# Delta net: block inverse issued in a row on VectorE, convolution taps and background products queued behind it, some key-query products in other PSUM banks

## The chip, the core and the metric

The kernel runs on one core of a Trainium2 chip. The core has five engines, each with a queue of its own that it works through in order: PE (TensorE, matmul; its weight loads are listed as PEld), DVE (VectorE), ACT (ScalarE), POOL (GpSimd) and SP (SyncE, which here issues most of the DMAs). An instruction that waits holds up everything behind it on its engine. The metric is the device time of the kernel in microseconds, the median of several executions.

## The reference

Two layers of a transformer trunk over 1024 positions of width 1024. The first layer's mixer is a gated delta net, the second's is retention; behind each stands a gated feed-forward block. The change touches the delta net alone:

```python
qkv = jax.nn.silu(causal_dwconv(qkv, conv_w))          # four taps
...
kk = jnp.where(strict, jnp.einsum('bhncd,bhnmd->bhncm', kb, k) * decay, 0.0)
eye = jnp.eye(C, dtype=F32)
rhs = jnp.concatenate([v * beta[..., None], kb * jnp.exp(gc)[..., None]], axis=-1)
sol = lax.linalg.triangular_solve(kk + eye, rhs, left_side=True, lower=True, unit_diagonal=True)
...
qk = jnp.where(causal, jnp.einsum('bhncd,bhnmd->bhncm', q, k) * decay, 0.0)
...
_, o = lax.scan(step, state0, xs)                       # state passed from chunk to chunk
```

There are 8 heads. For every head and chunk a unit lower triangular matrix has to be inverted (or solved with). Apart from that the layer is a large projection of the input (`h @ w_in`, 4112 columns), a convolution of four taps with a SiLU, key-query products and a scan over chunks.

## The kernel before

**The parts.** The kernel takes chunks of 128 positions, 8 of them. The delta net works on four pairs of heads. For each pair there are: `t_front` (decay and key-key products, which make the matrix `U`), `t_solve` (one for two pairs: inverts all 32 x 32 diagonal blocks of four heads at once), `t_chain` (joins the inverted blocks to inverses of 128 x 128 by small matmuls), `prep` (turns values and keys), `dt_half` (key-query products, multiplied by the decay that is loaded back from DRAM), and `scan`, one per head. Underneath lies `filler`: the projection matmuls, one unit of 128 columns after the other. A unit loads its weights (`load_w`, lines 100 to 106: a DMA into a raw tile `wr`, then ACT rounds it to `wh`, then DVE takes the rest into `wl`), runs 24 matmuls of 128 x 512 for each half of the positions (three for each of eight k tiles, the first of them with `wl`), and, for convolution units, calls `conv_half` on each half.

**Convolution.** `conv_half` (lines 443 to 456) copies the PSUM bank twice on ACT (lines 449 and 452), adds three taps on DVE (line 454) and applies SiLU on ACT (line 455). For query and key units, `ssq_late` comes some time later: it turns the finished features on PE (line 638) and sums their squares on ACT (line 473).

**Background.** `bg_step` at the end of a unit runs one piece of a matrix-vector product that a later stage needs: a DMA of 512 KB into a tile `mvw` and two products on DVE (lines 214 and 216, into `ada`). `mvw` and `wr` share one tag with two buffers, so a piece that waits for its products holds a buffer that raw weights need.

**The inverse.** `t_solve` (lines 785 to 818) copies the blocks into `X` on ACT (line 792), transposes them on DVE to `Y` (line 796), and then does 31 elimination steps, each a product (line 804, into `fs`) and a subtraction (line 806, into `T`), each depending on the one before: 62 instructions in a chain. Then follow the transpose `RX` on DVE (line 810), the reordering copy `TP` on ACT (line 812) and the transpose `TX` on DVE (line 814). `t_chain` copies `RX` into `R` (ACT line 852, POOL line 854) and `TX` into `T0` (ACT line 841). The loads of the decay tiles `DT` for `dt_half` (line 944) go into a buffer that `T` leaves.

**What sets the order.** PE's order in the delta net is written by hand: a small planner (`run`, lines 646 to 680) keeps a clock, advances it by a cost for each matmul, takes the ready stream with the best priority, and pins every matmul behind the one before (`pq`). A stream says by `yield LAT[...]` how long it thinks its work on other engines lasts. In `t_solve` it yields 1.9 us after every second elimination step, so that other streams are traced in between. The order on DVE, ACT, POOL and SP comes from a scheduler, which goes by the order of tracing and by its own estimate of when an operand is ready. `after(key)` (line 94) adds an edge for order only: what is traced inside it, on the same engine as the anchor instruction, is issued behind that instruction. It adds no wait.

**PSUM.** Eight banks: four of tag `acc`, two of `mm`, two of `sc`. `dt_half`, `prep`, `t_front` and `t_chain` use `mm`, the scans use `sc` and `acc`.

Of the kernel before, what the change touches and what calls it, by code (L numbers as in the profile page):

```python
# [12 lines left out]
ALU = mybir.AluOpType  # L13
# [3 lines left out]
D = 1024  # L17
# [16 lines left out]
def trunk_kernel(ctx: ExitStack, tc, A):  # L34
# [84 lines left out]
    def bg_step(tile=mm_tile):  # L119
        bg_ps[0] = tile  # L120
        if bg:
            bg.pop(0)()
# [38 lines left out]
    for k in range(KT):  # L161
        w = two("hTa", F32, "mvw")
# [17 lines left out]
    pt = col_sum([a0])  # L180
# [262 lines left out]
    def conv_half(tile_idx, acc, half, o, prev):  # L443
        raw = tl("cv", [P, 516], name="raw")
        if half == 0:
            pool.memset(raw[:, 0:3], 0.0)
        else:
            pool.tensor_copy(raw[:, 0:3], prev[:, HALF:HALF + 3])
        act.activation(raw[:, 3:515], acc, AF.Copy)
        w = gdn_cw[:, tile_idx * 4:tile_idx * 4 + 4]  # L450
        oh = o[half]
        act.activation(oh, acc, AF.Copy, scale=w[:, 3:4])  # L452
        for j in range(1, 4):
            dve.scalar_tensor_tensor(oh, raw[:, 3 - j:515 - j], w[:, 3 - j:4 - j], oh, ALU.mult, ALU.add)  # L454
        act.activation(oh, oh, AF.Silu)
        return raw

# [237 lines left out]
    def give(tag, n):  # L695
        free[tag] += n
# [88 lines left out]
    def t_solve(qd_):  # L785
        yield after_ev(("T0", 2 * qd_ - 1), ("A", 2 * qd_), ("A", 2 * qd_ + 1))
        yield from take("lane", 1)
        X = tl("lane", [P, 32, 32], name="X")
        for h in pairs[2 * qd_] + pairs[2 * qd_ + 1]:
            for b in range(4):  # L790
                bs = slice(32 * b, 32 * b + 32)
                act.activation(X[bs, :, h % 4 * 8:h % 4 * 8 + 8].rearrange("p i c -> p c i"), U[h][bs, :, bs], AF.Copy)
        yield from take("lane", 2)
        yield LAT["X"]
        Y = tl("lane", [P, 32, 32], name="Y")
        dve.transpose(flat(Y), flat(X))
        T = tl("lane", [P, 32, 32], name="T")
        pool.memset(T, 0.0)
        pool.memset(flat(T)[:, 0:1024:33], 1.0)
        tmp = tl("fs", [P, 256], name="fs")  # L800
        for j in range(31):
            ni, nj = 31 - j, j + 1
            tv = tmp[:, 0:ni * nj].rearrange("p (i j) -> p i j", j=nj)
            dve.tensor_tensor(tv, bc(Y[:, j + 1:, j], nj), bm(T[:, j, 0:nj], ni), ALU.mult)
            ts_ = T[:, j + 1:, 0:nj]
            dve.tensor_tensor(ts_, ts_, tv, ALU.subtract)
            if j % 2:
                yield LAT["fs"]
        RX = tl("lane", [P, 32, 32], name="RX")
        dve.transpose(flat(RX), flat(T))  # L810
        TP = tl("lane", [P, 32, 32], name="TP")
        act.activation(TP, T.rearrange("p i j -> p j i"), AF.Copy)
        TX = tl("lane", [P, 32, 32], name="TX")
        dve.transpose(flat(TX), flat(TP))
        RTX[qd_] = (RX, TX)
        give("lane", 1)
        emit(("Tq", qd_))
        emit(("T", qd_), LAT["T"])
# [111 lines left out]
    def dt_half(p, q4):  # L930
        heads = pairs[p]
        if q4 == 0:
            yield after_ev(("Tq", p // 2), ("M", p - 1))
            yield from take("lane", 1)
            t = tl("lane", [P, 2, HALF], name="DT")
            tiles = [t[:, 0], t[:, 1]]
        else:
            yield after_ev(("Tq", p // 2), ("S", p - 1))
            yield from take("auh", 2)
            emit(("Dt", p))  # L940
            tiles = [tl("auh", [P, HALF], name="DT") for _ in range(2)]
        for h, t in zip(heads, tiles):
            DT[h, q4] = t
            sp.dma_start(t, Ld[h][:, hs(q4)])
        yield LAT["ld"]
        for h, t in zip(heads, tiles):
            yield after_ev(("f", h))
            pt = mm_tile()
            for c in range(4):
                n = q4 * 4 + c  # L950
                pm(pt[:, c * P:(c + 1) * P], fx(GH + h, n), fx(h, n))
            dve.tensor_tensor(t, t, pt, ALU.mult)
            emit(("D", h, q4), LAT["D"])
            yield LAT["mm"]
# [92 lines left out]
    def filler(items):  # L1047
        spare = [(z, k) for k in range(GH)]
        todo = list(items)
        while todo or spare:  # L1050
# [34 lines left out]
            if kind == "c":  # L1085
                if ti < GH:
                    yield [(0.2, ssq_late(ti))]
                else:
                    emit(("f", ti), LAT["fv"])
            bg_step(acc_tile)  # L1090

    LAT = {"kk": 3.05, "ld": 1.14, "g1": 17.30, "gm": 2.50, "mm": 1.81, "T": 4.98, "X": 3.38, "fs": 1.9, "T0": 5.00, "t1": 1.65, "t2": 2.35, "t3": 1.34, "D": 2.67, "s1": 1.60, "s2": 1.22, "s3": 1.26, "tail": 12.31, "ssq": 9.30, "fv": 2.85}
# [829 lines left out]
```

## Time and profile before

| | |
|---|---|
| median of 3 runs | 3016.57 us (3015.99 to 3017.25) |
| the profiled execution | 3017.08 us, of which the profile's span is 3015.3 us |
| mean granted clock of PE | 0.975 |
| busy share of the span, VectorE | 73% (2196.9 us) |
| busy share of the span, ScalarE | 45% (1349.4 us) |
| DMA, mean rate | 147 GB/s |
| elimination steps (lines 804 and 806) | 62 instructions each, over both inverses |
| first inverse, start of first and last step | 178.9 and 222.1 us |
| second inverse, start of first and last step | 428.5 and 474.7 us |

The times of rows are counted from the start of the span. A row of the timeline gives start, duration, engine, line, operation, operands and the number of instructions merged, and in brackets how long the engine had been idle before it and what ended that idle time. A row of a window gives, for each engine, the busy time and in parentheses the number of instructions, then the granted clock of PE (1.00 is full speed), the DMA share and rate.

### The profile page before, as it was taken

Reading aid. Unit: us, or ns where it says so; the run is one execution under the profiler, and the core shown is the slowest. Engines: PE = TensorE matmul, PEld = TensorE weight load, DVE = VectorE, ACT = ScalarE, POOL = GpSimd, SP = SyncE. Lnnn points to the kernel's source line nnn. Section 1 sums busy time; section 2 is a strip of 40 time slices with the busy share of each in tenths; the row PEclk is TensorE's granted clock in tenths of the full one; section 3 lists DMA queues with packets and bytes.
Section 4 is the critical chain, followed back from the end, with each engine's and each line's share of the span. In section 5 each row is a group of like instructions: output and inputs, shape, how many; then the busy total and the mean of one; then the engine's idle time right before and its main releaser. Section 6 shows DMA issues by size and latency. Waiting matters only on the chain.

```text
span 3015.3 us, 38927 instructions
## 1 busy us (share of the span) xinstructions
PE 2843.1 (94%) x13638; PEld 2313.8 (77%) x13638; DVE 2196.9 (73%) x3845; ACT 1349.4 (45%) x2513; POOL 637.6 (21%) x629
## 2 busy tenths in 40 slices
PE   8889998999989999999999999989999899999997
PEld 7768877887768878777777787767777688888785
DVE  5795687545578888997688745556688787778888
ACT  4655555434544444536533343222336544445444
POOL 0411221133011111520023302522201011113503
PEclk9999999999999999999999999999999999999998
DMA  7222221343344444863423444656563333335652
GB/s 271 84 74 71 95 92 64 115 158 136 109 140 159 156 153 148 308 205 126 154 84 112 171 157 136 209 168 189 190 234 118 115 133 105 105 105 211 229 174 106
DMA packets 238708, 442.36 MB, mean 147 GB/s; under 512 B 22448, under 2 KB 75952, under 8 KB 238512
## 3 DMA queue, kind: packets, MB, share of 16 engines
q1 hardware_dynamic: 207328, 392.16, 38.6%
q10 hardware_dynamic: 29760, 43.00, 3.9%
q0 software_dynamic: 1424, 4.72, 0.4%
q8 instruction: 107, 1.75, 0.2%
q14 instruction: 89, 0.73, 0.1%
HBM read 331.26 MB, written 108.53 MB: 146 GB/s over the span
## 4 chain that ended last, share of the span: by engine, by line
PE 58%; DVE 16%; DMA 10%; issue 8%; ACT 4%; POOL 2%; SPq 1%; POOLq 0%; DVEq 0%; ACTq 0%
PE acc L635 14%; PE acc L1418 8%; PE acc L1157 6%; PE acc L110 4%; PE acc L111 4%; PE acc L112 4%; PE sc L1157 3%; PE sc L635 3%; PE mm L635 2%; PE sc L1418 2%; DVE ab L90 1%; PE sc L111 1%; PE sc L110 1%; PE sc L112 1%; DVE wb L90 1%
## 5 line engine op out<-in xcount | busy, mean ns | idle before, releaser
L1418 PE MATMUL acc<-bb,ab 128*128 128x512 f32 x1800 | 432.5, 393 | 7.7 <-DVE bb L90 5.8
L1418 PEld LDWEIGHTS acc<-bb,ab 128*128 128x128 f32 x1800 | 337.0, 189 | 85.0 <-DVE bb L90 10.3
L635 PE MATMUL acc<-hT,wh 128*128 128x512 f32 x960 | 302.6, 397 | 0.0
L1556 POOL TENSOR_TENSOR o<-o 128x512 f32<-128x512 f32 x88 | 119.0, 1363 | 723.8 <-DVE o L1549 716.1
L1157 PE MATMUL acc<-T,wb 128*128 128x512 f32 x840 | 209.6, 400 | 15.1 <-DVE wb L90 15.1
L635 PEld LDWEIGHTS acc<-hT,wh 128*128 128x128 f32 x960 | 184.2, 192 | 34.6
L635 PE MATMUL acc<-hT,wl 128*128 128x512 f32 x480 | 204.4, 426 | 0.2 <-ACT sg L1083 0.2
L1157 PEld LDWEIGHTS acc<-T,wb 128*128 128x128 f32 x840 | 160.6, 192 | 54.0 <-DVE wb L90 20.3
L90 DVE TENSOR_TENSOR ab<-ar,ab 128x512 fp32r<-128x512 f32 x210 | 179.4, 862 | 29.4 <-ACT ab L89 29.3
L89 ACT ACTIVATE ab<-ar 128x512 fp32r<-128x512 f32 x210 | 128.4, 623 | 134.3 <-PE acc L1418 73.3
L90 DVE TENSOR_TENSOR wb<-wr,wb 128x512 fp32r<-128x512 f32 x162 | 114.8, 711 | 100.1 <-ACT wb L89 97.3
L90 DVE TENSOR_TENSOR wl<-wr,wh 128x1024 fp32r<-128x1024 f32 x85 | 107.4, 1264 | 89.2 <-ACT wh L89 89.2
L89 ACT ACTIVATE wh<-wr 128x1024 fp32r<-128x1024 f32 x101 | 106.8, 1058 | 122.0 <-PE acc L635 55.7
L1214 ACT ACTIVATE pc<-acc 128x512 f32<-128x512 f32 x143 | 84.8, 593 | 169.5 <-PE acc L1157 98.6
L90 DVE TENSOR_TENSOR wb<-mm,wb 128x512 fp32r<-128x512 f32 x216 | 145.0, 684 | 21.2 <-ACT wb L89 19.2
L89 ACT ACTIVATE wb<-mm 128x512 fp32r<-128x512 f32 x216 | 122.5, 594 | 66.4 <-DVE mm L1203 66.3
L89 ACT ACTIVATE wb<-wr 128x512 fp32r<-128x512 f32 x162 | 98.8, 626 | 97.6 <-DMA wr<-in_ffn_up 51.3
L635 PE MATMUL acc<-wh,hT 128*128 128x512 f32 x384 | 137.1, 420 | 2.0 <-DVE vv L90 2.0
L1535 DVE SCALAR_TENSOR_TENSOR o<-g,vc,o 128x512 f32<-128x512 f32 (+2 forms) x176 | 135.8, 790 | 1.3 <-ACT o L1530 0.7
L454 DVE SCALAR_TENSOR_TENSOR qkv<-raw,vc,qkv 128x512 f32<-128x512 f32 x144 | 114.6, 800 | 25.9 <-ACT qkv L452 24.8
L89 ACT ACTIVATE bb<-Br 128x512 fp32r<-128x512 f32 x120 | 74.0, 624 | 123.1 <-DVE Br L1302 61.8
L110 PE MATMUL acc<-T,wb 128*128 128x512 f32 x292 | 116.3, 398 | 9.9 <-DVE wb L90 9.4
(618 smaller groups left out, 7148.3 us busy)
## 6 DMA issues: line engine op xcount, KB each, us to landing
wr<-in_ffn_up SPq DMA_DIRECT2D x96, 512.0 KB, 4.2
mvw<-in_ada_w SPq DMA_DIRECT2D x80, 512.0 KB, 4.4
ad<-o SPq DMA_DIRECT2D x154, 256.0 KB, 2.3
ar<-ad SPq DMA_DIRECT2D x154, 256.0 KB, 3.7
Br<-in_ffn_down SPq DMA_DIRECT2D x66, 256.0 KB, 3.9
wr<-in_ret_wv SPq DMA_DIRECT2D x32, 512.0 KB, 3.7
ar<-od SPq DMA_DIRECT2D x56, 256.0 KB, 4.4
xs<-xt ACTq DMA_DIRECT2D x24, 512.0 KB, 3.0
```

What stands on the lines that cost most here:

```text
L89: act.activation(dst_h, src, AF.Copy)
L90: eng.tensor_tensor(dst_l, src, dst_h, ALU.subtract)
L110: mm(acc, wl[:, k], hl[0], start=first, stop=False)
L111: mm(acc, wh[:, k], hl[1], start=False, stop=False)
L112: mm(acc, wh[:, k], hl[0], start=False, stop=last)
L454: dve.scalar_tensor_tensor(oh, raw[:, 3 - j:515 - j], w[:, 3 - j:4 - j], oh, ALU.mult, ALU.add)
L635: pq(pe.matmul(out, lhsT, rhs, start=start, stop=stop, **kw), cost)
L1157: return pe.matmul(*a, skip_group_check=True, **kw)
L1214: act.activation(t, X, AF.Copy)
L1418: mm_ = (lambda *a, p=p, onto=onto, **kw: (mm if p < 2 else pe.matmul)(*a, skip_group_check=onto, **kw))
L1535: dve.scalar_tensor_tensor(tv, gv[:, c0 - j:c1 - j], w[:, 2 - j:3 - j], tv, ALU.mult, ALU.add)
L1556: pool.tensor_tensor(o[d], o[x], o[y], op)
```

## The change

Four edits. The planner's `t_solve` no longer yields between elimination steps: all 62 are traced at once, and one yield of 27.0 us stands behind the transposes. The last subtraction becomes an anchor `inv`; the three taps of every convolution half, and every background step of `filler`, that are traced later stand behind it on DVE (the transposes, copies and DMAs of a background step are on other engines and are not held). The key-query product of `dt_half` takes a bank of tag `sc` instead of `mm` for the first half of the positions of the first and third pair.

```diff
@@ conv_half
         act.activation(oh, acc, AF.Copy, scale=w[:, 3:4])
-        for j in range(1, 4):
-            dve.scalar_tensor_tensor(oh, raw[:, 3 - j:515 - j], w[:, 3 - j:4 - j], oh, ALU.mult, ALU.add)
+        with after("inv"):
+            for j in range(1, 4):
+                dve.scalar_tensor_tensor(oh, raw[:, 3 - j:515 - j], w[:, 3 - j:4 - j], oh, ALU.mult, ALU.add)
         act.activation(oh, oh, AF.Silu)
@@ t_solve
             ts_ = T[:, j + 1:, 0:nj]
-            dve.tensor_tensor(ts_, ts_, tv, ALU.subtract)
-            if j % 2:
-                yield LAT["fs"]
+            anchor["inv"] = dve.tensor_tensor(ts_, ts_, tv, ALU.subtract)
         RX = tl("lane", [P, 32, 32], name="RX")
...
         RTX[qd_] = (RX, TX)
+        yield LAT["inv"]
         give("lane", 1)
@@ dt_half
-            pt = mm_tile()
+            pt = mm_tile() if p % 2 or q4 else sc_tile()
@@ filler
-            bg_step(acc_tile)
+            with after("inv"):
+                bg_step(acc_tile)
@@ LAT
-"fs": 1.9
+"inv": 27.0
```

Below is the built order of the instructions of both kernels. In the kernel with the change the line numbers from 455 to 807 are larger by one, 810, 812 and 814 become 809, 811 and 813, and those from there to the end of `filler` are the same. The number behind a tile's name tells one buffer's use from another.

**First inverse, VectorE.** Before, from the transpose `Y` on (`qkv` rows are taps, `ada` rows background products):

```order
L796 STREAM_TRANSPOSE Y_1461<-X_1426 128x1024
L216 SCALAR_TENSOR_TENSOR ada_1548<-mvw_1669,e_162,ada_1548 128x512
L454 SCALAR_TENSOR_TENSOR qkv_1471<-raw_1472,vc_153,qkv_1471 128x512
L804 TENSOR_TENSOR fs_1466<-Y_1461,T_1463 128x31
L454 SCALAR_TENSOR_TENSOR qkv_1471<-raw_1472,vc_153,qkv_1471 128x512
L806 TENSOR_TENSOR T_1463<-T_1463,fs_1466 128x31
L454 SCALAR_TENSOR_TENSOR qkv_1471<-raw_1472,vc_153,qkv_1471 128x512
L804 TENSOR_TENSOR fs_1466<-Y_1461,T_1463 128x60
```

With the change, the end of the same inverse (its 62 steps stand in a row, with one small instruction among them):

```order
L805 TENSOR_TENSOR fs_1466<-Y_1461,T_1463 128x31
L807 TENSOR_TENSOR T_1463<-T_1463,fs_1466 128x31
L455 SCALAR_TENSOR_TENSOR qkv_1535<-raw_1536,vc_153,qkv_1535 128x512
L455 SCALAR_TENSOR_TENSOR qkv_1591<-raw_1592,vc_153,qkv_1591 128x512
L214 TENSOR_SCALAR ada_1600<-mvw_1601,e_162 128x512
L809 STREAM_TRANSPOSE RX_1529<-T_1463 128x1024
L455 SCALAR_TENSOR_TENSOR qkv_1636<-raw_1637,vc_153,qkv_1636 128x512
L455 SCALAR_TENSOR_TENSOR qkv_1535<-raw_1536,vc_153,qkv_1535 128x512
L813 STREAM_TRANSPOSE TX_1533<-TP_1531 128x1024
L455 SCALAR_TENSOR_TENSOR qkv_1591<-raw_1592,vc_153,qkv_1591 128x512
L216 SCALAR_TENSOR_TENSOR ada_1600<-mvw_1601,e_162,ada_1600 128x512
```

The taps of the features 1535 and 1591, the first query unit traced after `t_solve`, moved from among the steps to behind the last one, and the first two of them and a background product stand ahead of `RX`.

**First inverse, PE.** The place in PE's order where these features are turned (`cst` is the identity), before:

```order
L635 MATMUL acc_1601<-hT_658,wh_1555 128x512 x2
L638 MATMUL acc_1632<-cst_155,qkv_1471 128x128 x4
L638 MATMUL acc_1642<-cst_155,qkv_1539 128x128 x4
L635 MATMUL acc_1601<-hT_674,wl_1556 128x512
L635 MATMUL acc_1601<-hT_674,wh_1555 128x512 x2
L635 MATMUL acc_1679<-hT_280,wl_1676 128x512
```

and with the change:

```order
L636 MATMUL acc_1645<-hT_658,wh_1607 128x512 x2
L639 MATMUL acc_1668<-cst_155,qkv_1535 128x128 x4
L639 MATMUL acc_1678<-cst_155,qkv_1591 128x128 x4
L636 MATMUL acc_1645<-hT_674,wl_1608 128x512
L636 MATMUL acc_1645<-hT_674,wh_1607 128x512 x2
L636 MATMUL acc_1711<-hT_280,wl_1708 128x512
```

PE's order did not move at this place: the same transposes stand behind the same number of matmuls in both.

**First inverse, ScalarE.** The copies around `TP` (`qkv<-qkv` is a SiLU, `wh<-wr` the rounding of new weights), before:

```order
L455 ACTIVATE qkv<-qkv 128x512 x2
L449 ACTIVATE raw<-acc 128x512
L452 ACTIVATE qkv<-acc,vc 128x512
L89 ACTIVATE wh<-wr 128x1024
L455 ACTIVATE qkv<-qkv 128x512
L812 ACTIVATE TP<-T 128x1024
L852 ACTIVATE R<-RX 32x4x32 x12
L841 ACTIVATE T_1857<-TX 32x8x32 x6
```

and with the change:

```order
L811 ACTIVATE TP<-T 128x1024
L852 ACTIVATE R<-RX 32x4x32 x12
L841 ACTIVATE T_1833<-TX 32x8x32 x6
L456 ACTIVATE qkv<-qkv 128x512 x2
L89 ACTIVATE wh<-wr 128x1024
```

The SiLUs of 1535 and 1591 and the rounding of the next weights moved from ahead of `TP` to behind the copies into `R` and `T0`.

**Second inverse, VectorE.** Weights of the second unit behind the start of the inverse, before (inside the steps):

```order
L804 TENSOR_TENSOR fs_3916<-Y_3911,T_3913 128x112
L454 SCALAR_TENSOR_TENSOR qkv_3947<-raw_3948,vc_153,qkv_3947 128x512
L90 TENSOR_TENSOR wl_4062<-wr_4059,wh_4061 128x1024
L806 TENSOR_TENSOR T_3913<-T_3913,fs_3916 128x28x4
```

and with the change (behind the last step; on ScalarE the rounding that this needs stands behind the copies into `R` and `T0`, ahead of the SiLUs):

```order
L807 TENSOR_TENSOR T_3913<-T_3913,fs_3916 128x31
L455 SCALAR_TENSOR_TENSOR qkv_4003<-raw_4004,vc_153,qkv_4003 128x512
L214 TENSOR_SCALAR ada_4012<-mvw_4013,e_162 128x512
L455 SCALAR_TENSOR_TENSOR qkv_4048<-raw_4049,vc_153,qkv_4048 128x512
L809 STREAM_TRANSPOSE RX_3979<-T_3913 128x1024
...
L216 SCALAR_TENSOR_TENSOR ada_4012<-mvw_4091,e_162,ada_4012 128x512
L90 TENSOR_TENSOR wl_4098<-wr_4095,wh_4097 128x1024
```

The `wl` of that unit moved from the fourth elimination step to fifteen instructions behind the last. Here three taps, of features 3895, still stand among the first four steps.

More of the change, by code (lines that the diff above doesn't have):

```diff
@@ L1089, in filler @@
                     emit(("f", ti), LAT["fv"])
-            bg_step(acc_tile)
-    LAT = {"kk": 3.05, "ld": 1.14, "g1": 17.30, "gm": 2.50, "mm": 1.81, "T": 4.98, "X": 3.38, "fs": 1.9, "T0": 5.00, "t1": 1.65, "t2": 2.35, "t3": 1.34, "D": 2.67, "s1": 1.60, "s2": 1.22, "s3": 1.26, "tail": 12.31, "ssq": 9.30, "fv": 2.85}
+            with after("inv"):
+                bg_step(acc_tile)
+    LAT = {"kk": 3.05, "ld": 1.14, "g1": 17.30, "gm": 2.50, "mm": 1.81, "T": 4.98, "X": 3.38, "inv": 27.0, "T0": 5.00, "t1": 1.65, "t2": 2.35, "t3": 1.34, "D": 2.67, "s1": 1.60, "s2": 1.22, "s3": 1.26, "tail": 12.31, "ssq": 9.30, "fv": 2.85}
     pairs = [(2 * p, 2 * p + 1) for p in range(GH // 2)]
```

## The prediction

> **What bounds the kernel now.** First the page: which engine is full?
>
> ```profile
> span 3015.3 us, 38927 instructions
> PE 2843.1 (94%) x13638; PEld 2313.8 (77%) x13638; DVE 2196.9 (73%) x3845; ACT 1349.4 (45%) x2513; POOL 637.6 (21%) x629
> ```
>
> PE is busy for 94% of the span, so the time is PE's work plus PE's idle time, and a change that alters no matmul can win or lose only what it does to the idle time. The profiled execution took 3017.08 us, 1.8 outside its span and 0.5 above the median; I sum against it and take 0.5 off.
>
> Second, the windows around the two inverses: where in the delta net is PE idle?
>
> ```profile
> 191.50:240.00 48.50, 34.02 (x227) 28.22 (x226) 39.99 (x84) 24.16 (x60) 5.94 (x19) 0.85 0.13 44
> 240.00:426.00 186.00, 176.44 (x1304) 150.52 (x1303) 125.47 (x343) 103.13 (x222) 42.61 (x56) 0.98 0.24 84
> 426.00:453.20 27.20, 27.20 (x126) 22.59 (x125) 26.09 (x54) 11.33 (x19) 1.32 (x6) 1.00 0.39 130
> 453.20:490.00 36.80, 24.83 (x239) 20.72 (x240) 26.99 (x60) 22.40 (x71) 6.82 (x16) 0.86 0.17 58
> 490.00:620.00 130.00, 124.87 (x994) 108.53 (x989) 73.18 (x172) 60.63 (x157) 11.17 (x19) 0.97 0.30 102
> ```
>
> The columns are stretch, length, then PE, PEld, DVE, ACT, POOL, granted clock, DMA. PE is idle 48.50 − 34.02 = **14.5 us** behind the first inverse and 36.80 − 24.83 = **12.0 us** behind the second. While the second inverse runs (426 to 453) it is not idle at all, though DVE is full there (26.09 of 27.20).
>
> Third, PE's timeline: what ends these waits?
>
> ```profile
> 191.48 1.03 PE L638 MATMUL acc<-cst,qkv 128*128 128x128 f32 x8
> 209.60 2.42 PE L635 MATMUL mm<-qkv 128*128 128x128 f32 x16 [1.22 <-DVE qkv L917]
> 212.80 0.65 PE L638 MATMUL mm<-cst,qkv 128*128 128x128 f32 x4 [0.78 <-DVE DT L952]
> 214.33 0.63 PE L638 MATMUL mm<-cst,qkv 128*128 128x128 f32 x4 [0.88 <-DVE qkv L917]
> 228.04 2.07 PE L635 MATMUL mm<-qkv 128*128 128x128 f32 x8 [11.14 <-DVE DT L952]
> 463.84 0.66 PE L638 MATMUL mm<-cst,qkv 128*128 128x128 f32 x4 [1.69 <-DVE DT L952]
> 470.36 1.16 PE L635 MATMUL mm<-qkv 128*128 128x128 f32 x8 [1.35 <-DVE qkv L917]
> 480.42 2.07 PE L635 MATMUL mm<-qkv 128*128 128x128 f32 x8 [8.90 <-DVE DT L952]
> ```
>
> Two waits carry it, 11.14 and 8.90 us: the planner takes an inverse for shorter than it is, and PE's row then reaches key-query products whose decay tile cannot be loaded until `T` is done. The others are turns of the two `mm` banks.
>
> **Part 1: the inverse itself.** Without taps between them, how long do 62 steps take? Busy time of lines 804 and 806 over the first inverse, then of each over a stretch where they already stand in a row:
>
> ```profile
> 178.90:222.50 43.60, 10.52 (x31) 0.96 0.23 73
> 178.90:222.50 43.60, 10.58 (x31) 0.96 0.23 73
> 216.42:222.31 5.89, 2.63 (x9) 0.70 0.00 1
> ```
>
> 18 steps (the last row is the same for both lines) are busy 5.26 us in 5.89, so 0.035 us lie between two. 62 steps: 21.1 + 62 × 0.035 = **23.3 us**, against 43 and 46 now.
>
> The Trainium skill ("VectorE: DVE Perf Modes", "The DRAIN you can't avoid") says that a pipeline flush of about the operation's duration less 266 ns follows each operation, which chaining cannot avoid; that speaks against a long row of dependent ones. By it, at a mean of 0.34 us, some 0.07 us each or 4.6 us an inverse would come on top (an estimate from that page), and the sum would be 9 us higher. The 0.035 measured in a row is half of that and already counted.
>
> Start of the first one:
>
> ```profile
> 169.05 0.16 DVE L230 SCALAR_TENSOR_TENSOR v<-cs,vc 128x4 f32<-128x4 f32 x1
> 169.13 0.48 DVE L214 TENSOR_SCALAR ada<-mvw,e 128x512 f32<-128x512 f32 x1
> 172.42 1.12 DVE L781 SCALAR_TENSOR_TENSOR U<-mm,cj,U 128x128 f32<-128x128 f32 x4
> 173.63 2.78 ACT L792 ACTIVATE X<-U 32x256 f32<-32x256 f32 x4 [1.84 <-DVE U L781]
> 177.62 0.71 DVE L216 SCALAR_TENSOR_TENSOR ada<-mvw,e,ada 128x512 f32<-128x512 f32 x1
> 178.24 0.75 DVE L454 SCALAR_TENSOR_TENSOR qkv<-raw,vc,qkv 128x512 f32<-128x512 f32 x1
> 178.91 0.20 DVE L804 TENSOR_TENSOR fs<-Y,T 128x31 f32<-128x31 f32 x1
> ```
>
> Background products and taps between 169.05 and 172.42 leave, so `U` comes over 2 us sooner; ACT waited 1.84 for it, so `X` and `Y` gain 1.84, and one product (177.62 to 178.24) goes from ahead of the first step. It starts at 178.91 − 1.84 − 0.62 = 176.45 and ends at **199.75** instead of 222.3.
>
> The second:
>
> ```profile
> 427.87 0.74 DVE L216 SCALAR_TENSOR_TENSOR ada<-mvw,e,ada 128x512 f32<-128x512 f32 x1
> 428.53 0.21 DVE L804 TENSOR_TENSOR fs<-Y,T 128x31 f32<-128x31 f32 x1
> ```
>
> `X` waits for nothing that moves, one product goes, three taps stay among the steps at 0.67 each (178.24 to 178.91): 427.87 + 23.3 + 2.0 = **453.2** instead of 474.9. Both inverses end some 22 us sooner, and the waits of 11.14 and 8.90 go. What is late next?
>
> **Part 2: what stands behind it, first inverse.** PE reaches the transposes of 1535 at 191.48, as before: nothing ahead of them in its row moved, and their weights are split before the inverse. But their taps now stand behind the inverse, and their SiLU on ACT behind the copies into `R` and `T0`.
>
> ```profile
> 203.68 0.63 ACT L455 ACTIVATE qkv<-qkv 128x512 f32<-128x512 f32 x1 [2.34 <-DVE qkv L454]
> 222.33 1.96 ACT L812 ACTIVATE TP<-T 128x1024 f32<-128x1024 f32 x1 [11.46 <-DVE T L806]
> 224.19 5.13 ACT L852 ACTIVATE R<-RX 32x128 f32<-32x128 f32 x12
> 229.35 3.99 ACT L841 ACTIVATE T<-TX 32x256 f32<-32x256 f32 x6
> 222.33 1.25 DVE L810 STREAM_TRANSPOSE RX<-T 128x1024 f32<-128x1024 f32 x1
> ```
>
> Two taps and a background product (0.67 + 0.67 + 0.48) precede `RX`, 1.25: ready at 199.75 + 1.8 + 1.25 = 202.8. `TP` ends sooner. Then 5.13 and 3.99 of copies, 0.63 of SiLU: **212.6**. The third tap of 1535 ends near 208, hidden by the copies. PE is idle from 191.5 to 212.6: **21.1 us**. The next weights follow on ACT and DVE (SiLU, 1.06, 1.22 below: 215.5), while PE does eight transposes and three matmuls at its restart clock; hidden.
>
> **Second inverse.** Here no transpose comes first, but weights do.
>
> ```profile
> 420.59 31.98 PE acc L635 x141
> 434.43 1.22 DVE L90 TENSOR_TENSOR wl<-wr,wh 128x1024 fp32r<-128x1024 f32 x1
> 443.54 1.06 ACT L89 ACTIVATE wh<-wr 128x1024 fp32r<-128x1024 f32 x1
> 481.96 3.96 ACT L841 ACTIVATE T<-TX 32x256 f32<-32x256 f32 x6
> DMA to landing us min/median/max: 3.4/3.5/3.9
> ```
>
> A matmul takes 31.98 / 141 = 0.227. From 420.59 PE has 96 with weights split before the inverse, until **442.4**. `wl_4098` stands behind the inverse and needs `wh`, which on ACT stands behind the copies: 453.2 + 1.8 + 1.25 (`RX`) + 5.13 + 3.96 + 1.06 + 1.22 = **467.6**. Beside it, the raw weights wait for the `mvw` buffer that the held products free near 458.4 (453.2, then four taps, two products and `RX`), and 3.5 for landing: 461.9, hidden. PE is idle **25.2 us**.
>
> **The sum.** After the restart the inverse is done, so only turns of banks remain, 0 to 3 us a window (2.9 and 3.0 now); with `sc` banks sharing the key-query products I take 1, and this is all I grant that edit. Each window has one long restart in both kernels (2.07 us for eight small matmuls, twice a normal rate), which cancels. First: 21.1 + 1 − 14.5 = +7.6. Second: 25.2 + 1 − 12.0 = +14.2. Outside these windows the same matmuls and steps stand in almost the same row: 0, between −6 and +5, since 240 to 426 holds 9.6 us of idle time and 490 to 620 5.1, of which half could go. Total **+21.8**: 3017.1 + 21.8 − 0.5 = **3038**.
>
> Bounds: without the gaps between steps 2.2 less a window, with three bank turns 2 more, without the earlier start 1.8 more; +5 to +11.5 and +11 to +17. With the rest +10 to +33; their middle gives 3029 to 3047.
>
> **Rivals.** (A) *The waits simply go.* If PE had other work until the release, the two waits of 20.0 us and their restarts, about 2 each, would go: 3016.6 − 24 = 2993. It is decided by the time of the release: a gain needs it before 191.5 + 14.5 = 206.0 and 442.4 + 12.0 = 454.4. The steps end at 199.75 and 453.2, in time; what speaks against is the 13 to 14 us of copies and splits behind them in rows that are fixed. For it speaks only that a wait I overlooked delays PE's arrival.
>
> (B) *One wait for another, at the same price.* Without the copies into `R` and `T0` on the path (9.1 us), the releases would come with the third tap and its SiLU (208.6) and with the landed weights and their splits (461.9 + 1.06 + 1.22 = 464.2): +3.6 and +10.8. If besides all the 14.7 us of idle time elsewhere went, because the inverse is there sooner, the sum would be 3016, within 0.2% of now (0.2%, 6 us, is about what a measurement can tell from no change). Against it stands ACT's row, which has the copies ahead.
>
> (C) *The buffers run on.* Held products keep a `wr` buffer, so the weights behind the first late ones are late too: 3.5 + 1.06 + 1.22 = 5.8 us after the split, against 48 × 0.227 = 10.9 us of matmuls. Hidden; if `mvw` transfers or held taps take the difference, up to 6 us a window: 3050.
>
> (D) *The change doesn't do what it says.* The order shows one small instruction in the first row and three taps in the second; priced above.
>
> **Chances.** Forecast 0.74, A 0.09, B 0.11, C 0.06. Faster by over 0.2%: 0.09; within: 0.11; slower: 0.80. The range takes in most of B, the forecast's own, and stops short of A and C: 3015 to 3048.
>
> **What would show it.** In the changed profile the 62 steps last 23 to 24 us, no wait on `DT` (line 952 in both kernels) exceeds 3 us, PE waits some 21 us on a SiLU near 191 and some 25 us on `wl` near 450, and the ACT row shows the copies between. Wrong would be: PE busy through 191 to 212, the release before the copies, or a wait of over 5 us elsewhere in 240 to 620.

## The result, and the profile after

| | before | with the change |
|---|---|---|
| median | 3016.57 us (5 runs, 3010.43 to 3018.69) | 3029.25 us (5 runs, 3025.56 to 3032.55) |
| ratio | | 1.0044, 95% interval 1.0026 to 1.0061 |
| the profiled execution | 3017.08 us | 3030.25 us |
| PE idle in the delta net (table below) | 41.1 us | 62.9 us |

The change makes the kernel 12.7 us slower. Timed once more beside the later experiments, 12 runs gave 1.0035 (1.0021 to 1.0049). The page of the profiled execution with the change:

```profile
span 3028.5 us, 38920 instructions
PE 2832.7 (94%) x13638; PEld 2309.2 (76%) x13638; DVE 2211.0 (73%) x3845; ACT 1350.8 (45%) x2515; POOL 640.4 (21%) x629
```

The span grew by 13.2 us, and PE's busy time fell by 10.4 for the same 13638 matmuls. Both will matter: PE waits longer, and the same work takes it less time. Now the windows around the two inverses (length, then PE, PEld, DVE, ACT, POOL, clock, DMA), with the stretch ahead of the first, where PE was full before:

```profile
150.00:191.50 41.50, 36.87 (x181) 30.69 (x179) 37.82 (x127) 22.12 (x54) 5.96 (x9) 1.00 0.10 29
191.50:240.00 48.50, 30.38 (x251) 25.80 (x253) 35.03 (x56) 24.55 (x54) 9.54 (x18) 0.79 0.29 87
240.00:426.00 186.00, 173.27 (x1257) 148.76 (x1250) 122.83 (x331) 101.00 (x219) 41.11 (x55) 0.97 0.26 83
426.00:453.20 27.20, 23.13 (x105) 18.82 (x103) 24.45 (x70) 11.84 (x25) 3.41 (x7) 0.97 0.07 20
453.20:490.00 36.80, 15.89 (x64) 13.01 (x65) 25.48 (x45) 19.03 (x45) 9.30 (x16) 0.65 0.32 100
490.00:620.00 130.00, 127.80 (x1123) 112.06 (x1122) 79.51 (x177) 63.17 (x177) 10.09 (x20) 0.99 0.30 100
```

PE is idle 4.6 + 18.1 = 22.7 us at the first inverse (14.5 before), 4.1 + 20.9 = 25.0 at the second (12.0 before), and 12.7 + 2.2 = 14.9 in the two long stretches (14.7 before). PE's timeline at the places where it waited for `DT` before:

```profile
186.25 0.61 PE L636 MATMUL acc<-hT,wh 128*128 128x512 f32 x2
208.07 1.97 PE L639 MATMUL acc<-cst,qkv 128*128 128x128 f32 x8 [21.21 <-ACT qkv L456]
...
228.53 1.16 PE L636 MATMUL mm<-qkv 128*128 128x128 f32 x8 [0.68 <-DVE DT L952]
230.99 0.66 PE L639 MATMUL mm<-cst,qkv 128*128 128x128 f32 x4 [0.86 <-DVE DT L952]
...
474.11 0.80 PE L636 MATMUL acc<-hT,wl 128*128 128x512 f32 x1 [24.99 <-DVE wl L90]
```

The waits of 11.14 and 8.90 us on `DT` have become 0.68 and 0.86 in the first window, and the second has none worth a row. Two new ones stand there, on a SiLU and on a weight tile. What released them, on DVE (first and last steps, transpose, weight split) and on ACT:

```profile
171.52 0.20 DVE L805 TENSOR_TENSOR fs<-Y,T 128x31 f32<-128x31 f32 x1
195.14 0.19 DVE L807 TENSOR_TENSOR T<-T,fs 128x31 f32<-128x31 f32 x1
196.97 1.24 DVE L809 STREAM_TRANSPOSE RX<-T 128x1024 f32<-128x1024 f32 x1
434.73 0.20 DVE L805 TENSOR_TENSOR fs<-Y,T 128x31 f32<-128x31 f32 x1
459.52 0.19 DVE L807 TENSOR_TENSOR T<-T,fs 128x31 f32<-128x31 f32 x1
472.83 1.23 DVE L90 TENSOR_TENSOR wl<-wr,wh 128x1024 fp32r<-128x1024 f32 x1 [1.39 <-ACT wh L89]
```

```profile
198.24 5.20 ACT L852 ACTIVATE R<-RX 32x128 f32<-32x128 f32 x12 [0.80 <-DVE RX L809]
203.45 3.92 ACT L841 ACTIVATE T<-TX 32x256 f32<-32x256 f32 x6
207.39 1.15 ACT L456 ACTIVATE qkv<-qkv 128x512 f32<-128x512 f32 x2
471.75 1.06 ACT L89 ACTIVATE wh<-wr 128x1024 fp32r<-128x1024 f32 x1
```

The first inverse takes 171.52 to 195.33, 23.8 us, the second 434.73 to 459.71, 25.0. Behind the first one stand taps and a product, `RX`, 5.20 and 3.92 us of copies, and then the SiLU for which PE has waited since 186.86.

### The profile page after: what moved, and what is told of

Same layout as the page of the kernel before. It is cut to its first block, busy times and chain, and to the rows that moved or that the text cites. A ratio compares the mean times of both kernels' runs of the same rounds, so it can differ in the third digit from the quotient of the medians.

```text
span 3028.5 us, 38920 instructions
## 1 busy us (share of the span) xinstructions
PE 2832.7 (94%) x13638; PEld 2309.2 (76%) x13638; DVE 2211.0 (73%) x3845; ACT 1350.8 (45%) x2515; POOL 640.4 (21%) x629
## 4 chain that ended last, share of the span: by engine, by line
PE 56%; DVE 17%; issue 11%; DMA 9%; ACT 5%; POOL 3%; SPq 0%; POOLq 0%; ACTq 0%; DVEq 0%
PE acc L636 14%; PE acc L1419 7%; PE acc L1158 5%; PE sc L636 4%; PE acc L110 4%; PE acc L111 3%; PE acc L112 3%; PE sc L1158 3%; PE sc L1419 2%; PE mm L636 2%; DVE ab L90 1%; DMA wr<-in_ffn_up 1%; DVE bb L90 1%; PE sc L111 1%; DMA mvw<-in_ada_w 1%
## 5 line engine op out<-in xcount | busy, mean ns | idle before, releaser
L636 PE MATMUL acc<-hT,wl 128*128 128x512 f32 x480 | 205.5, 428 | 25.2 <-DVE wl L90 25.0
L1158 PE MATMUL acc<-T,wb 128*128 128x512 f32 x840 | 208.8, 398 | 15.8 <-DVE wb L90 15.8
L1158 PEld LDWEIGHTS acc<-T,wb 128*128 128x128 f32 x840 | 160.1, 192 | 54.9 <-DVE wb L90 21.5
L216 DVE SCALAR_TENSOR_TENSOR ada<-mvw,e,ada 128x512 f32<-128x512 f32 x140 | 108.2, 773 | 34.1 <-DMA mvw<-in_ada_w 33.9
L455 DVE SCALAR_TENSOR_TENSOR qkv<-raw,vc,qkv 128x512 f32<-128x512 f32 x144 | 115.1, 808 | 21.9 <-ACT qkv L452 20.9
```

Source lines behind the costliest of these rows:

```text
L216: dve.scalar_tensor_tensor(a, wr[:, kk], e[:, k:k + 1], a, ALU.mult, ALU.add)
L636: pq(pe.matmul(out, lhsT, rhs, start=start, stop=stop, **kw), cost)
L1158: return pe.matmul(*a, skip_group_check=True, **kw)
```

## The experiments

All runs together first, since they are read by the same three numbers. The "stretch" is the delta net, 3298 matmuls long: from one fixed matmul (the 561st in PE's row, ahead of everything that the change moves) to the first of line 315, the output projection. In the last three rows of the table it is counted by the same number of matmuls, but 16, 12 and 12 of them belong to the output projection, which there starts before the last matmuls of the delta net; those three rows compare less exactly. A window over just that stretch, for the kernel before and with the change:

```profile
148.03:662.60 514.57, 473.43 (x3300) 403.01 (x3299) 352.75 (x883) 268.81 (x617) 90.24 (x136) 0.96 0.27 91
```

```profile
143.23:677.61 534.38, 471.44 (x3301) 403.21 (x3299) 359.45 (x883) 271.25 (x619) 96.60 (x136) 0.94 0.27 88
```

Length less PE busy is PE's idle time: 41.1 and 62.9 us.

| run | time to before (95% interval) | stretch, us | PE idle in it | PE busy in it |
|---|---|---|---|---|
| before, three profiles | 1 | 514.6, 520.0, 523.4 | 41.1, 40.1, 43.2 | 473.4, 479.9, 480.3 |
| with the change, two profiles | 1.0044 (1.0026 to 1.0061), 1.0035 (1.0021 to 1.0049) | 534.4, 531.9 | 62.9, 63.0 | 471.4, 469.0 |
| row only | 1.0021 (1.0006 to 1.0037) | 524.5 | 51.7 | 472.8 |
| taps behind | 1.0071 (1.0050 to 1.0093) | 542.6 | 68.5 | 474.0 |
| products behind | 1.0093 (1.0070 to 1.0115) | 549.4 | 78.6 | 470.8 |
| both behind, no sc banks | 1.0073 (1.0053 to 1.0094) | 542.3 | 68.6 | 473.7 |
| before, with sc banks | 1.0030 (1.0014 to 1.0046) | 527.9 | 55.4 | 472.5 |
| change, copies last | 1.0045 (1.0030 to 1.0061) | 532.3 | 62.5 | 469.7 |
| before, longer step cost | 0.9992 (0.9977 to 1.0008) | 513.2 | 36.3 | 476.9 |
| z units under the inverse | 1.0023 (1.0010 to 1.0037) | 528.2 | 53.6 | 474.5 |
| z units, steps alone | 0.9976 (0.9963 to 0.9989) | 510.8 | 34.1 | 476.6 |

Against the mean of the three profiles of before (519.3), the stretch accounts for most of the measured times: with the change +13.8 (mean of two) against 12.7 and some 11 measured, products behind +30.1 against 28, z units with the steps alone −8.6 against −7. It does not with the longer step cost: −6.1, while the time stayed the same. A stretch is one execution, a time the median of several.

**Row only.** Which part of the change makes the stalls?

```diff
@@ conv_half
-        with after("inv"):
+        if True:
             for j in range(1, 4):
@@ dt_half
-            pt = mm_tile() if p % 2 or q4 else sc_tile()
+            pt = mm_tile()
@@ filler
-            with after("inv"):
-                bg_step(acc_tile)
+            bg_step(acc_tile)
```

> The kernel with the change, but taps and background products are not put behind the inverse, and all key-query products use the mm banks as before: what is left is that the steps are traced in a row, with one yield of 27.0. In the built order 29 other VectorE rows stand between the first and the last step of the first inverse (31 before, 1 with the change) and 42 of the second (39 and 3), so the steps are not in a row. Theory (the loss comes from what is queued behind the inverse): the waits of 21.2 us on a SiLU and of 25.0 us on a weight tile are gone, waits of about 10 us on the decay tile are back, and the time is that of before within 5 us (3012 to 3022). Rival (the planner's other order, through tracing in a row and the new yield, costs the time by itself): 3025 to 3035.

PE's two costliest groups of waits, by what ended them (us in total, times, longest):

```profile
PE mm L636 <- ACT T L841: 17.9, 2, 17.0
PE mm L636 <- DVE DT L952: 13.4, 1, 13.4
```

Neither new stall appears; the first inverse takes 42.2 us and the second 49.8, so tracing in a row alone doesn't issue in a row. The time lies in the theory's range (3019.75), but not all of it is as the theory said: one wait is on `DT`, the other, longer one on `T0`. The other planning costs something by itself, about 0.2%.

**Taps behind, and products behind.** Each anchor alone, both with `mm` banks:

```diff
@@ filler (taps behind)
-            with after("inv"):
-                bg_step(acc_tile)
+            bg_step(acc_tile)
@@ conv_half (products behind)
-        with after("inv"):
+        if True:
             for j in range(1, 4):
```

> The kernel with the change, but only the taps are put behind the inverse, not the background products, and all key-query products use the mm banks. In the built order 6 rows stand among the steps of the first inverse (4 background products, one weight split, one small one) and 11 of the second (6 products, 3 taps, 2 weight splits). Theory: in the first inverse the transposes near 190 still wait for a SiLU behind the inverse and the copies; the inverse is longer by 4 x 0.48 + 1.22 = 3.1 us, so 21 to 25 us of wait. In the second inverse two more units have their weights (2 x 10.9 us of matmuls), so the wait of 25.0 us on a weight tile falls below 10 us. Together 3018 to 3028, faster than the change by some 5 us. Rival (any wait of the one sort is only handed to the other): both windows stay as long as with the change, 3027 to 3035.

> The kernel with the change, but only the background products are put behind the inverse, not the taps, and all key-query products use the mm banks. 12 taps stand among the steps of each inverse (12 x 0.67 = 8.0 us), no weight split does; the next splits stand behind RX and some products. Theory: no wait of over 5 us on a SiLU, but in both windows PE waits for a weight tile behind an inverse that lasts 31 us instead of 23: from about 193 and from about 442 to 450, 25 to 33 us each. So slower than the change though less is queued behind the inverse: 3035 to 3055. Rival (the taps are what costs, since the SiLU wait vanishes): 3010 to 3020.

With the taps behind:

```profile
PE acc L639 <- ACT qkv L456: 51.7, 2, 28.6
```

With the products behind:

```profile
PE acc L636 <- DVE wl L90: 57.1, 2, 29.5
```

Taps behind: 3036 us, where 3018 to 3028 was expected, a miss. The weight wait of the second window is gone as expected, but PE runs on only to the transposes of features whose taps stand behind that inverse, and waits 23.1 us there: one wait was handed to the other, as the rival said. The first wait grew to 28.6 us (21 to 25 expected), so the time lies above the rival's range (3027 to 3035) too. Products behind: 3043 us, with waits of 27.6 and 29.5 us on weight tiles, as expected. With 12 taps among its steps the inverse takes 31 us, and the weights stand behind that longer inverse. Against the change with the same banks (the next runs, 3036 us), holding the taps alone back won nothing, and holding the products alone back cost some 7 us (1.0093 against 1.0073; the intervals overlap, but the stretch is 7 us longer and the idle time 10). What counts is when the first thing that PE needs comes out of the row.

**The banks.** The change without its bank edit, and the kernel before with it alone:

```diff
@@ dt_half (both behind, no sc banks)
-            pt = mm_tile() if p % 2 or q4 else sc_tile()
+            pt = mm_tile()
@@ dt_half (before, with sc banks)
-            pt = mm_tile()
+            pt = mm_tile() if p % 2 or q4 else sc_tile()
```

> The kernel with the change, but all key-query products use the mm banks as before. Theory (the banks are worth only the turns of two mm banks, 0 to 3 us a window): the waits of 21 and 25 us stay, and the time is that of the change plus 0 to 5 us, 3029 to 3035. Rival (the banks gave back the 9 us by which the change came out below the forecast): 3036 to 3042.

> The kernel before with only the last edit: the key-query products of the first half of the positions of the first and third pair take sc banks. Theory (that edit is worth the turns of the two mm banks, and gave the change some 7 us in the stretch behind its inverses): the waits of 11.1 and 8.9 us on DT stay within 3 us of that, since they wait for the decay tile and not for a bank, and the time falls by 2 to 8 us to 3008 to 3014. Rival (it is worth something only where the steps stand in a row): 3014 to 3019.

A row of the change without the bank edit:

```profile
527.75 0.45 PE L639 MATMUL mm<-cst,qkv 128*128 128x128 f32 x1 [3.97 <-DVE R L905]
```

The waits of the kernel before with it:

```profile
PE mm L635 <- ACT T L841: 36.9, 4, 17.6
```

Without it the change takes 3036 us, just inside the rival's range: beside the new row order the banks are worth some 7 to 9 us (3036.2 against 3029.25 and 3027.53; stretch 542.3 against 534.4 and 531.9), of which 5.6 are idle time. The largest single wait among them, 3.97 us, comes 48 us after the second release, where a `prep` transpose waits for an `mm` bank that `t_chain` still holds. Alone, the same edit costs 0.30%, which neither side had: PE's waits move from `DT` (20.0 us) to `T0` (36.9), and the inverses take 51.6 and 50.9 us instead of 43.4 and 46.4. More taps and other rows stand among the steps there: the planner's order changed with the banks. The edit isn't worth a fixed sum of its own.

**Copies last.** Are the copies into `R` and `T0` on the path of both releases?

```diff
@@ ahead of split
+    held = {"s": 2, "w": 2}
@@ conv_half
-        act.activation(oh, oh, AF.Silu)
+        s = act.activation(oh, oh, AF.Silu)
+        if held["s"] < 2:
+            held["s"] += 1
+            anchor["s"] = s
@@ split
-        act.activation(dst_h, src, AF.Copy)
+        h = act.activation(dst_h, src, AF.Copy)
+        if held["w"] < 2:
+            held["w"] += 1
+            anchor["wh"] = h
@@ t_solve
         RTX[qd_] = (RX, TX)
+        held["s"] = held["w"] = 0
@@ t_chain (around the ACT copies into T0, and those into R)
+        first_ = {0: "s", 2: "wh"}.get(p)
...
+                with after(first_):
...
+                      with after(first_):
```

> The kernel with the change, and one thing more: on ScalarE the copies into T0 and R of the pair that comes first behind each inverse are issued behind the SiLU (first inverse) and behind the rounding wh of the late weights (second inverse) instead of ahead of them; four copies into R of another pair stay ahead. Theory (these copies, 9.1 us, stand on the path of both releases): the first release comes with the third tap, near 204.3 instead of 208.1, so the wait on the SiLU falls from 21.2 to 16 to 18 us; the second comes with the landing of the raw weights plus wh, two taps and wl, so the wait falls from 25.0 to 19 to 22 us; the time falls by 6 to 9 us to 3020 to 3024. Rival (the copies are only pushed behind, and PE waits for T0 or R later): the two waits shorten but a new one of 4 us or more appears on T0 or R, 3027 to 3033.

PE's rows in this run:

```profile
208.43 0.48 PE L647 MATMUL acc<-cst,qkv 128*128 128x128 f32 x1 [17.70 <-ACT qkv L461]
217.12 0.79 PE L644 MATMUL acc<-hT,wl 128*128 128x512 f32 x1 [5.44 <-DVE wl L95]
475.78 0.80 PE L644 MATMUL acc<-hT,wl 128*128 128x512 f32 x1 [22.88 <-DVE wl L95]
```

The first wait falls from 21.2 to 17.7 us (16 to 18 expected) and the second from 25.0 to 22.9 (19 to 22 expected), so the copies were on both paths. But the next weights, whose rounding now stands behind the copies, make PE wait 5.44 us more, and the time is that of the change (1.0045). The rival's outcome, at another place than it said.

**Before, longer step cost.** Is before's idle time only a number in its planner?

```diff
@@ LAT (kernel before)
-"fs": 1.9
+"fs": 2.9
```

> The kernel before with one number changed: the planner counts 2.9 us instead of 1.9 for every second elimination step, near to what the trace of before shows (43 us for 30 of them and the rest). Theory (the idle time of before comes from a planner that takes the inverse for too short): the waits of 11.1 and 8.9 us on DT shrink below 4 us each and the time falls to 3000 to 3010. Rival (more filler means more taps among the steps, so the inverse only gets longer; in the built order 54 and 44 rows stand among the steps instead of 31 and 39): the waits stay over 6 us, 3012 to 3022.

The longest wait on `DT` falls to 5.1 us (below 4 by the theory, over 6 by the rival) and the idle time by some 5, yet the time does not change (0.9992), which is the rival's outcome. As the rival said, more filler means more taps among the steps: the inverses take 60.5 and 52.8 us. Only this one value was tried.

**Units without taps under the inverse.** If the loss is that PE reaches what stands behind the inverse, PE should be given work that needs nothing from DVE: the units of the `z` gate.

```diff
@@ filler (from the kernel with the change)
+    under = [None]
+    owed = [0]
+
+    def busy():
+        return under[0] is not None and under[0] not in events
...
-            if not todo or (todo[0][0] == "c" and free["qkv"] < 2 and len(spare) > 4):
+            if not todo or (todo[0][0] == "c" and free["qkv"] < 2 and len(spare) > 4) or (busy() and spare):
...
-            w = load_w(A["gdn_wqkv" if kind == "c" else "gdn_wz"][ti])
+            w = load_w(A["gdn_wqkv" if kind == "c" else "gdn_wz"][ti], eng=pool if busy() else dve)
...
-            with after("inv"):
-                bg_step(acc_tile)
+            if busy():
+                owed[0] += 1
+            else:
+                for _ in range(1 + min(1, owed[0])):
+                    bg_step(acc_tile)
+                owed[0] = max(0, owed[0] - 1)
@@ t_solve
         RTX[qd_] = (RX, TX)
+        under[0] = ("Tq", qd_)
@@ ssq_late
         yield LAT["ssq"]
+        if busy():
+            yield after_ev(under[0])
```

> The kernel with the change, but while the planner counts an inverse as under way its filler takes units of the z gate (no convolution, so no taps; the split wl is done on GpSimd) and leaves their background steps for later units, and the transposes of features wait for the end of the inverse in the planner. The steps of an inverse have 10 and 9 other rows among them. Theory (the loss is PE reaching things that stand behind the inverse, and the idle time of before is the same inverse seen from the other side): neither wait of over 5 us is left in either window, the 20 us of waits on DT of before do not come back, and the time is 2990 to 3005, below both kernels. Rival (the filler that is used up here is missing at the end of the delta net, where the scans then stand alone): waits of 10 us and more on scan products between 500 and 660, 3010 to 3030.

```profile
PE acc L639 <- ACT qkv L456: 21.0, 1, 21.0
PE mm L639 <- ACT qkv L456: 12.6, 1, 12.6
```

A miss: 3023 us, still slower than before. These waits (the groups of this run) show why: products and a weight split had slipped among the steps, the inverses took 36.7 and 33.9 us, and the planner, counting 27, sent PE to the held transposes too soon. So both were mended:

```diff
@@ filler (further)
-            w = load_w(A["gdn_wqkv" if kind == "c" else "gdn_wz"][ti], eng=pool if busy() else dve)
+            with after("inv"):
+                w = load_w(A["gdn_wqkv" if kind == "c" else "gdn_wz"][ti], eng=pool if busy() else dve)
...
-                    bg_step(acc_tile)
+                    with after("inv"):
+                        bg_step(acc_tile)
@@ ssq_late
             yield after_ev(under[0])
+            yield LAT["ssq"]
```

> As the run with units of the z gate under the inverse, and three things more: the weight splits on VectorE and the background steps of the filler stand behind the inverse too, so that in the built order its 62 steps have no other row among them, and transposes of features wait 9.3 us longer in the planner after the inverse. In the run before it waits of 20.95 and 12.64 us were left, in a delta-net stretch of 528.1 us (matmul 560 to matmul 3858 of the row). Theory (what costs is only what PE reaches while it stands behind the inverse): each inverse takes 23 to 24 us, no wait of over 5 us is left, the stretch falls to 492 to 502 us (before 514.6, with the change 534.4) and the time to 2994 to 3004, below both kernels. Rival (the idle time only moves on, to T0, R or the scans at the end): one or more new waits of over 5 us, stretch 508 to 525, time 3008 to 3024.

```profile
PE sc L636 <- ACT w L981: 6.3, 10, 1.5
PE mm L639 <- ACT qkv L456: 5.3, 1, 5.3
```

This version is faster than both kernels, if only by 0.24% against the one before: 3009.98 us, 0.9976 (0.9963 to 0.9989). Time and stretch are the rival's (3008 to 3024, 508 to 525), not the theory's (2994 to 3004, 492 to 502), and so is one wait of over 5 us, 5.3. The stretch, 510.8, is longer than the theory's for two reasons: PE's idle time went down only to 34.1 us, in many short waits on the scans (the first row: ten of at most 1.5 us) and on banks, and each inverse took 27.5 to 28 us, not 23 to 24. For that see the last section.

**The unchanged kernels, profiled again.**

> The kernel before, unchanged, profiled once more, to see how much one execution differs from another in the parts that the change can't reach. Theory (the 7 us between the sum of the delta-net stretch, +19.8, and the measured +12.7 are the spread of single executions outside that stretch): the stretch from matmul 560 to 3858 stays at 514.6 within 2 us, while the parts ahead of it (148.0) and behind it (2352.7) differ by 2 to 6 us. Rival (the change makes the rest faster): the parts outside stay within 1 us, and the delta-net stretch also.

> The kernel with the change, unchanged, profiled and timed once more beside the others. Theory: delta-net stretch 534.4 within 2 us, the part ahead of it 143.2 to 149, the part behind it 2345 to 2357; the median 3027 to 3034, 12 to 18 us above before. Rival (the change makes the rest faster): the part ahead of it again 143 and the part behind it again 2 us shorter than in before.

> The kernel before, unchanged, profiled a third time. In its first profile the clock was granted at half speed for 4.6 us after the second long wait (the wait ended at 480.4, the full clock came at 485.0), in its second profile for 19.8 us (478.1 to 497.9), and the delta-net stretch took 514.6 and 523.4 us. Theory (how long the half clock lasts after that wait differs from one execution to the next, and makes the stretch): a third value of the half clock, and a stretch of 514 us plus about half of what it lasts over 4.6; all other pieces of the stretch within 0.5 us, or differing by single steps of the clock. Rival (one of the two profiles was an exception of another kind): the stretch differs with the same half clock.

The theory of the first of these runs was right outside the stretch, where the parts differ by 2 to 6 us, and fell inside it: the stretch of the kernel before did not stay at 514.6 within 2 us, it took 523.4 and 520.0 in two further executions, with nearly the same idle time (43.2 and 40.1 for 41.1). The change's second stretch, 531.9, missed its range by half a microsecond; its median, 3027.5, lies in its range. The part ahead of the stretch took 148.0, 143.8 and 143.1 us before and 143.2 and 146.6 with the change; the part behind it 2352.7, 2356.1 and 2356.2 before and 2350.9 and 2351.2 with the change. Why the part behind comes out some 4 us shorter with the change wasn't studied and stays open.

Taken 150 matmuls at a time, most pieces of the stretch agree within 0.2 us between the three executions. Most of the difference stands at one place, behind the second wait. First the kernel before as first profiled, then its second profile, then its third (clock third from the end):

```profile
478.00:484.00 6.00, 3.58 (x14) 3.39 (x15) 3.86 (x6) 5.82 (x14) 4.65 (x12) 0.50 0.50 172
484.00:490.00 6.00, 6.00 (x136) 4.72 (x137) 0.08 (x1) 3.90 (x7) 0.00 (x0) 0.92 0.00 0
490.00:495.00 5.00, 5.00 (x76) 4.17 (x71) 4.31 (x13) 1.40 (x2) 0.00 (x0) 1.00 0.02 3
```

```profile
478.00:484.00 6.00, 5.94 (x52) 5.19 (x53) 2.08 (x4) 5.39 (x10) 2.52 (x7) 0.50 0.22 83
484.00:490.00 6.00, 6.00 (x55) 4.61 (x52) 0.00 (x0) 1.38 (x3) 0.00 (x0) 0.50 0.00 0
490.00:495.00 5.00, 5.00 (x99) 4.55 (x94) 2.52 (x7) 2.04 (x3) 0.00 (x0) 0.50 0.01 3
495.00:500.00 5.00, 5.00 (x39) 4.02 (x38) 3.46 (x8) 0.58 (x1) 0.00 (x0) 0.71 0.17 35
```

```profile
476.10:484.00 7.90, 7.88 (x80) 7.08 (x81) 2.07 (x3) 5.66 (x11) 2.33 (x7) 0.50 0.19 66
484.00:490.00 6.00, 6.00 (x103) 4.67 (x103) 0.74 (x1) 3.03 (x5) 0.00 (x0) 0.61 0.01 3
```

The wait ends at 480.4, 478.1 and 476.1. In the first execution the clock is full again about 1 us behind 484; in the second it stays at half until 497 or so, though PE is busy all the time. This place alone holds 6.6 of the 8.8 us between the two; in the third execution the half clock ends near 489, and 3.4 of 5.5 us stand here. That is a third value of the half clock, as the theory of that run had it; by its sum the stretch would have taken 518, not 520.0, and the rest stands in a few pieces that differ by up to 1.1 us. With the change, PE restarts behind its second wait with another kind of work:

```profile
474.00:478.00 4.00, 3.89 (x9) 3.11 (x10) 1.56 (x3) 0.72 (x2) 0.00 (x0) 0.50 0.54 173
478.00:482.00 4.00, 4.00 (x17) 3.18 (x17) 2.38 (x3) 0.69 (x1) 0.00 (x0) 0.89 0.67 188
```

Here the clock is full again within 5 us, and likewise in the second profile.

## Why the prediction was right, and where a size was off

**The inverse.** Right: 23.8 and 25.0 us for 23.3 and 25.3 forecast. The estimate of 4.6 us more an inverse, from the flush that the Trainium skill ("VectorE: DVE Perf Modes", "The DRAIN you can't avoid") gives for each operation, did not come true here.

**What is late next.** Right: a SiLU behind the copies at the first, `wl` behind `wh` behind the copies at the second, and waits of 21.2 and 25.0 us for 21.1 and 25.2. From the end of the inverse to the release it took 12.7 and 14.4 us; the forecast's steps give 12.85 and 14.4. Taps behind and products behind show each cause by itself. That the next weights are hidden behind the first release was right for the change, but holds only while the copies delay that release itself; with the copies last they cost 5.4 us.

**The idle time.** +8.2 and +13.0 us in the windows, for +7.6 and +14.2; +0.2 in the rest, for 0. Over the whole stretch idle time rose by 21.8 in the two profiles that were compared, and by 21.5 between the means of all: the sum of +21.8 was the idle time. That the rest came to 0 is luck, by way of the banks. "This is all I grant that edit", 2 us a window, was at the wrong place and too little: in the windows the run without it has the same 47.7 us of idle time, and outside them 5.7 more, which would have put the rest at +5.9, past the forecast's bound of +5.

**The restart.** This is the term that was mis-sized: "Each window has one long restart in both kernels, which cancels." With it fell the premise at the head of the prediction, that a change which alters no matmul can win or lose only idle time. PE's busy time for the same matmuls is 473.4, 479.9 and 480.3 us before and 471.4 and 469.0 with the change, on average 7.7 us less. 21.5 less 7.7 is 13.8, and 12.7 was measured.

Most of the 7.7 is clock. By the clock records of the five traces, PE was busy at half clock for 22.1, 37.9 and 37.1 us of the stretch before and for 22.9 and 17.7 with the change: 12.1 less on average, worth half of that, 6.0 us. Behind the first wait the restart does cancel (4.3 to 5.7 us at half clock before, 4.6 and 5.9 with the change). Behind the second it lasted 4.6, 12.6 and 19.8 us before and 4.8 and 5.0 with the change, which makes 3.7 of the 7.7 us; another 2.3 lie in spells of half clock elsewhere in the stretch, and 1.7 us are not clock and stay open.

The forecast had seen one execution of before, and in that one the restart behind the second wait happened to be the shortest of three; its total was near the median only because the part ahead of the delta net was the longest of three (148.0). Between the two first profiles the busy time differs by only 2.0 us and the stretch by 19.8; the span grew by 13.2 because the part ahead was 4.8 us shorter and the part behind 1.8.

A cause that fits all five profiles is the kind of matmul that follows: behind the second wait of before, 64 matmuls of 32 x 32 come some 4 us after the restart, where otherwise 128 x 512 ones do. No run changed only that, so it is argued and not shown.

**The rivals.** A, the waits simply going, needed a release within 14.5 and 12.0 us of PE's arrival; it came 21.2 and 25.0 us behind that, in both windows too late. B did not happen either: its total, 3016, needed the copies off the path and all idle time elsewhere gone, but the copies stood on both paths, and elsewhere 14.9 us stayed of 14.7. That its terms for the two windows alone, +3.6 and +10.8, lie near the measured +12.7 is chance, since the waits were the forecast's; and with the copies last the time stayed that of the change (1.0045). C did not happen: no wait on weights over 5 us followed either release. D fell with the profile: the steps took 23.8 and 25.0 us.

## What to carry to other kernels

Before work is put behind a long chain on one engine, find the first instruction of the busiest engine that needs something from that queue, and count from the end of the chain through every in-order queue in between; holding back less can be worse if it makes the chain longer. Here such a chain paid only with work beside it that needs nothing from its engine, and with a planner that knows the chain's length nearly: both together turned +0.4% into −0.24%. And price idle time and clock apart: a wait costs its length once and a restart afterwards, whose length one profile shows only as a sample.

## What the runs showed of the hardware

**The clock after a wait.** Behind a wait of 9 us the same matmuls ran at half clock for some 5, 13 and 20 us in three executions of one kernel. The Trainium skill ("TensorE: Matmul & The Clock Gate", "Part 1: The HAM clock gate (the "warmup" mystery)") says that the full clock comes after one sustained busy window of about 3.4 us. The restarts of some 5 us fit that if the window can begin at any time behind the wait; those of 13 and 20 us, with PE busy throughout, don't.

**VectorE and GpSimd.** In the last version nothing stands among the 62 steps, yet the inverse took 27.6 us instead of 23.8. The timeline of that run, with the rows of the other engines left out:

```profile
181.28 0.39 DVE L805 TENSOR_TENSOR fs<-Y,T 128x220 f32<-128x220 f32 x1
...
181.60 2.39 POOL L90 TENSOR_TENSOR wl<-wr,wh 128x1024 fp32r<-128x1024 f32 x1 [6.11 <-ACT wh L89]
...
181.70 2.53 DVE L807 TENSOR_TENSOR T<-T,fs 128x220 f32<-128x220 f32 x1
...
184.27 0.40 DVE L805 TENSOR_TENSOR fs<-Y,T 128x231 f32<-128x231 f32 x1
```

The step that meets the weight split on GpSimd takes 2.53 us instead of 0.39: it stands still for the whole split. Two splits an inverse cost some 4.2 us, more than the same splits would on VectorE itself (1.23 each). The Trainium skill ("SBUF — State Buffer", "Who interferes with whom") says that the two engines share a port pair with an exclusive lock, held for the whole instruction; these rows agree.
